# Turning q as plain values and splitting it behind the turn, with q and k-and-v tiles in alternation

## The chip, the core and the metric

The kernel runs on one core of a Trainium2 chip. A core has a matrix engine (TensorE, in the profile PE, with its weight loads as PEld), a vector engine (VectorE, DVE), an engine for activation functions and copies (ScalarE, ACT), a general-purpose engine (GpSimd, POOL) and one that issues transfers (SyncE, SP). They run side by side and wait for each other through semaphores. Data lie in SBUF (128 partitions); TensorE writes its results to PSUM, from where ScalarE and VectorE read them. The metric is the time of one execution on the device, in microseconds (us). Each instruction of one execution was recorded by the hardware profiler; that record is the trace, and its summary the profile page.

## The reference, cut to what matters

One encoder layer for 1024 tokens of 1024 channels, in float32: a half-step feed-forward block, then attention and a state-space part (SSD) side by side on the same projection, an output projection, a second feed-forward block and a gated embedding, each with a layer norm. The change touches the projection to q, k and v, and the normalisation and rotation of q and k:

```python
u = x @ w_in[i]
q, k, v, z, xs, bm, cm, dt_raw = jnp.split(u, SPLIT_POINTS, axis=-1)
qf = _rms(q.reshape(B, S, N_Q_HEADS, HEAD_DIM).astype(jnp.float32), q_norm[i])
kf = _rms(k.reshape(B, S, N_KV_HEADS, HEAD_DIM).astype(jnp.float32), k_norm[i])
qh = _apply_rope(qf, cos, sin).astype(x.dtype)
kh = _apply_rope(kf, cos, sin).astype(x.dtype)
vh = v.reshape(B, S, N_KV_HEADS, HEAD_DIM)
att_out = _block_attention(qh, kh, vh)
```

There are 8 q heads and 2 k and v heads of 64 channels; `_rms` divides each head of each token by its root mean square, and `_apply_rope` turns pairs of channels by an angle that depends on the token. `xs`, `bm` and `cm` (the x/B/C part) go through a short convolution and into the SSD part.

## The kernel before

**Precision.** A float32 product is computed as three products of a shorter type (`F32R`): each operand is split into a leading part hi (a rounded copy) and the rest lo (the difference), and lo-hi, hi-lo and hi-hi are added in PSUM (`mm3`, L116 to L123). `split_into` (L107) makes such a pair: a copy on ScalarE (L108) and a subtraction on VectorE (`lo`, L87). Both run for every weight block and every activation that goes into a product.

**Memory.** PSUM is used through two pools of buffers: `big`, two buffers of 1024 columns (`psb`, L41 and L55), and `sm`, four buffers of 512 (`pss`). A tile that is asked for waits until a buffer of its pool is free, which is when all that read it have run. Split weight blocks live in `ring` (ten buffers, L46). Raw weights land in `raw` buffers, of which there are two in this stage (L1606), by a DMA that SP issues (L94).

**Order.** The whole kernel is traced under `in_order` for TensorE (L1932): its instructions run in the order in which the program names them. On the other engines a scheduler chooses the order at compile time, except where `behind(engine)` ties what follows behind the last instruction named so far on that engine.

**The stage.** Just ahead of it `z_part` computes six tiles of z and loads and splits the q weights (`q_weights`). `qkv_part` (L841) then works in tiles of 128 tokens, t = 0 to 7. The q loop calls `qq(t)`: 24 matmuls of 512 columns into an `sm` buffer. The k-and-v loop calls `kv(t)`: 24 matmuls of 272 columns (128 of k, 128 of v, 16 of dt). After each product comes `step`, which does three things: it takes the oldest waiting *turn* from the list `late`, if more than `keep` of them wait (1 in the q loop, 2 in the k-and-v loop); it runs the *front* of this tile; and it runs the *back* of the tile before.

- `norm` (L862), in the front of both: a square on ScalarE (L865), a sum over each head on VectorE (L867), a scale and an added constant (L868), and the power -1/2 on GpSimd (L870).
- `rope` (L873), in the back: a Newton step for the root (L129 to L132), the product with it (L877, the last reader of the `sm` buffer), and the rotation (L883 to L886) with tables `T`. The tables are products of cosine and sine with the norm's weights, made on VectorE (L859); k's take the place of q's after the first k-and-v tile.
- `q_back` (L920): the rotated q is split into `qs`, per head 64 columns of hi beside 64 of lo (ScalarE L923, VectorE L87). Its turn transposes the 8 heads, 128 x 128 each, so that hi lies over lo in the partitions, into one `big` buffer (L929), and a copy of 1024 columns takes it to `Q` (L930).
- `kv_back` (L904): `rope` writes k twice side by side into `kn`; the turn transposes the 2 heads into an `sm` buffer (L911), and a copy (L913) and a subtraction (L87) split them into `K`.

Attention then multiplies `Q` (hi over lo) with `K`'s hi and lo (L1192). Behind the two loops, `xbc_gemm(0)` computes x0, the first of eight blocks of the x/B/C part, into a `big` buffer, in two halves of 24 matmuls; after each half two of the four steps in `pend` run (L960), which work off the turns that are left. `xbc_part` then reads x0 in a convolution (L992, L997) and goes on with x1 (L1002), into a `big` buffer again. The k-and-v weights are loaded and split in two parts (`kv_weights`, L812) with the last two q tiles, into `ring`; those of x/B/C in `xbc_weights` (L964), at their use.

## Time and profile before

| | |
|---|---|
| time, three runs | median 1938.63 us (1938.40 to 1939.19) |
| the profiled execution | 1938.82 us |
| its span, first to last instruction | 1937.0 us |
| mean granted clock of TensorE | 0.998 |
| transposes of q (L929) | 64, each 272 ns by the trace, from 718.7 to 759.5 us |
| transposes of k (L911) | 16, each 272 ns, from 762.7 to 784.3 us |

The span runs from the first to the last instruction; the rest of the execution's time, 1.8 us, lies around it. Times in the trace count from the span's start. A matmul's duration is longer than the distance to the next one's start, since matmuls overlap; what a group costs is read from the chain, where the pieces follow each other without overlap. Rows of groups give line, engine, operation, output and input with their shapes and count, then busy us and mean ns of one, then the idle time in front of them and what ended it. Rows of a timeline give start, length, engine, line and operation, and in brackets the idle time in front. In the rows of one line or tile, the three numbers are the least, median and greatest duration in ns.

### The profile page before, as it was taken

The page shows a single profiled execution, that of the slowest core. Times are in us where ns is not written, and L with a number is a line of the kernel's source. Part 1 is how long each engine was busy: PE and PEld are TensorE (multiplying, and loading weights), DVE is VectorE, ACT ScalarE, POOL GpSimd, SP SyncE. Part 2 cuts the span into 40 slices and gives each one's busy share as a digit, 9 for nine tenths or more (in the row PEclk, how much of TensorE's full clock was granted, in tenths as well). Part 3 has the DMA queues.
Part 4 walks back from the last instruction along what each step waited for, and adds up shares of the span by engine and source line. Part 5 has one row for each costly group of instructions (what it writes and reads, how often), then busy time and mean ns, then how long its engine had stood idle before and what let it go on. Part 6 is the DMA issues. An engine that isn't in the chain of part 4 may idle for free.

```text
span 1937.0 us, 25655 instructions
## 1 busy us (share of the span) xinstructions
PE 1926.7 (99%) x9130; PEld 1605.8 (83%) x9130; DVE 1524.2 (79%) x2362; ACT 877.5 (45%) x1502; POOL 418.2 (22%) x308
## 2 busy tenths in 40 slices
PE   9999999999999999999999999999999999999998
PEld 7888888888888889888888888888888888888886
DVE  7977777767678658758998888997787686877698
ACT  7433333334444224538897877633333333444311
POOL 0144544430001032001131001014444540001011
PEclk9999999999999999999999999999999999999999
DMA  8434554549866111241002663254544539976022
GB/s 307 134 127 156 189 186 147 196 155 392 279 218 219 61 44 47 88 126 63 6 1 90 218 211 126 92 173 144 184 177 165 188 118 358 333 261 224 27 78 97
DMA packets 147713, 310.34 MB, mean 160 GB/s; under 512 B 18128, under 2 KB 30800, under 8 KB 147584
## 3 DMA queue, kind: packets, MB, share of 16 engines
q1 hardware_dynamic: 147584, 308.69, 45.6%
q8 instruction: 72, 1.18, 0.3%
q14 instruction: 57, 0.47, 0.1%
HBM read 217.21 MB, written 91.42 MB: 159 GB/s over the span
## 4 chain that ended last, share of the span: by engine, by line
PE 99%; DVE 1%; DVEq 0%; issue 0%; ACT 0%
PE sm L122 56%; PE big L519 12%; PE sm L519 9%; PE big L122 6%; PE big L1192 3%; PE sm L1214 3%; PE sm L1229 2%; PE sm L1230 1%; PE sm L639 1%; PE sm L1410 1%; PE sm L1309 1%; PE sm L1320 1%; PE big L224 0%; PE big L929 0%; PE sm L224 0%; PE big L1725 0%
## 5 line engine op out<-in xcount | busy, mean ns | idle before, releaser
L122 PE MATMUL sm<-xh,blk 128*128 128x512 f32 x1424 | 439.8, 389 | 0.0
L122 PEld LDWEIGHTS sm<-xh,blk 128*128 128x128 f32 x1424 | 267.3, 188 | 55.3
L122 PE MATMUL sm<-xl,blk 128*128 128x512 f32 x736 | 283.8, 389 | 0.0
L122 PE MATMUL sm<-blk,xl 128*128 128x512 f32 (+2 forms) x704 | 208.1, 369 | 0.0
L108 ACT CAST blk<-raw 128x512 fp32r<-128x512 f32 (+1 forms) x168 | 101.1, 611 | 216.5 <-PE sm L122 135.3
L87 DVE TENSOR_TENSOR blk<-raw,blk 128x512 fp32r<-128x512 f32 (+1 forms) x168 | 141.6, 846 | 52.2 <-ACT blk L108 51.8
L108 ACT CAST blk<-s 128x512 fp32r<-128x512 f32 x172 | 105.7, 622 | 153.5 <-PE sm L122 126.0
L87 DVE TENSOR_TENSOR blk<-s,blk 128x512 fp32r<-128x512 f32 x176 | 141.8, 809 | 40.6 <-ACT blk L108 38.5
L178 POOL TENSOR_TENSOR ln_k<-ln_k,mhalf 128x1 f32<-128x1 f32 x32 | 37.8, 1185 | 578.2 <-DVE ln_k L177 562.0
L122 PEld LDWEIGHTS sm<-xl,blk 128*128 128x128 f32 x736 | 138.1, 188 | 28.8
L122 PE MATMUL sm<-blk,xh 128*128 128x512 f32 (+2 forms) x448 | 158.1, 373 | 0.0
L122 PEld LDWEIGHTS sm<-blk,xl 128*128 128x128 f32 x704 | 127.8, 188 | 20.8
L267 POOL TENSOR_TENSOR s<-raw 128x512 f32<-128x512 f32 x34 | 57.8, 1701 | 382.0 <-DVE blk L87 355.0
L519 PE MATMUL big<-xh 128*128 128x512 f32 x576 | 138.8, 390 | 0.0
L87 DVE TENSOR_TENSOR xh<-blk,xh 128x1024 fp32r<-128x1024 f32 x78 | 95.3, 1222 | 50.8 <-ACT xh L465 43.3
L465 ACT CAST xl<-blk 128x1024 fp32r<-128x1024 f32 x76 | 80.2, 1055 | 113.2 <-PE sm L519 45.1
L465 ACT CAST xh<-blk 128x1024 fp32r<-128x1024 f32 x78 | 82.2, 1054 | 107.1 <-PE big L519 45.4
L87 DVE TENSOR_TENSOR xl<-blk,xl 128x1024 fp32r<-128x1024 f32 x76 | 92.8, 1221 | 43.3 <-ACT xl L465 38.1
L519 PEld LDWEIGHTS big<-xh 128*128 128x128 f32 x576 | 107.8, 188 | 22.3
L519 PE MATMUL big<-xl 128*128 128x512 f32 x480 | 115.7, 390 | 0.0
L122 PE MATMUL sm<-xET2h,blk 128*128 128x512 f32 x352 | 108.3, 389 | 0.0
L122 PE MATMUL sm<-xET3h,blk 128*128 128x512 f32 x352 | 108.3, 389 | 0.0
(358 smaller groups left out, 4112.4 us busy)
## 6 DMA issues: line engine op xcount, KB each, us to landing
raw<-in_wi_dram SPq DMA_DIRECT2D x81, 512.0 KB
blk<-hS SPq DMA_DIRECT2D x154, 256.0 KB
hS<-h SPq DMA_DIRECT2D x88, 256.0 KB
wr<-in_wo_dram SPq DMA_DIRECT2D x44, 512.0 KB
blk<-wT SPq DMA_DIRECT2D x88, 256.0 KB
hS<-sg SPq DMA_DIRECT2D x66, 256.0 KB
wT<-wr SPq DMA_DIRECT2D x66, 256.0 KB
blk<-in_wo_dram SPq DMA_DIRECT2D x66, 256.0 KB
```

The costliest lines, as they stand in the source:

```text
L87: (eng or self.nc.vector).tensor_tensor(out=out, in0=full, in1=hi.bitcast(F32), op=ALU.subtract)
L108: self.nc.scalar.copy(out=b[:, 0, :n], in_=src)
L122: self.nc.tensor.matmul(ps, lhsT=a, rhs=b, start=(i == 0), stop=(i == n - 1))
L178: nc.gpsimd.tensor_tensor(out=r, in0=v, in1=self.mhalf[:, :1], op=ALU.pow)
L267: lambda: G.tensor_tensor(out=s1, in0=a21, in1=a22, op=ALU.add),
L465: A.copy(out=b[:, :, 0], in_=r)
L519: nc.tensor.matmul(ps[q], lhsT=b[:, 0, x, cut], rhs=b[:, 1, y], start=j == i == 0, stop=j == NP - 1 and i == 2)
L639: nc.tensor.matmul(o, lhsT=pT[t // 4][k][:, i, c], rhs=we[n][k][:, j], start=k + i + j == 0, stop=k + i == 2)
L1192: nc.tensor.matmul(ps[:, n * 512:(n + 1) * 512], lhsT=Q[:, h, q0:q0 + P], rhs=K[:, h // 4, j, n * 512:(n + 1) * 512], start=j == 0, stop=j ...
L1214: nc.tensor.transpose(out=pt[:, k], in_=pr[:, kk * P:(kk + 1) * P], identity=self.ident)
L1229: nc.tensor.matmul(po, lhsT=vw, rhs=pth[k // 4][:, k % 4], start=k == 0, stop=False)
L1230: nc.tensor.matmul(po, lhsT=vw, rhs=ptl[k // 4][:, k % 4], start=False, stop=k == KD - 1)
```

## The change

- `q_back` no longer splits in front of the turn. The turn transposes the plain rotated q, two heads (2 x 64 channels) at a time, into half of a `big` buffer: four transposes. Behind it, two ScalarE copies of 64 partitions round the even and the odd heads into `Q`, and two subtractions on VectorE write lo into the other 64 partitions. For odd heads lo lies over hi; the sum over the partitions in attention is the same.
- `norm` for q makes eight squares of one head each, with the sum from ScalarE's accumulator; VectorE's sum goes. For k it stays.
- The two loops become one: tile t of q, then tile t of k and v. `step` keeps 1 throughout; without a front it does nothing where no turn waits.
- k's turn takes a `big` buffer in place of an `sm` one.
- k's tables are made in front of the loop, on GpSimd, in place in the cosine and sine tables.
- `kv_weights` runs in front of the loop, in three loads of 3, 3 and 2 blocks; six blocks lie in a pool of their own (`wkvp`), two in `ring`.
- The weights of x0 are loaded and split in front of q's last step, behind what ScalarE and VectorE have been given by then; those of x1 behind the loop in the same way.
- Buffer counts: `qn` of q 4 (was 2), `kn` 2 (was 4), `qs` gone, k's square and rotation in small tiles of their own.

```diff
@@ -809,13 +809,11 @@
         self.nc.sync.dma_start(out=t, in_=self.I[key].broadcast_to([P, n]))
         return t
 
-    def kv_weights(self, part):
-        if part == 0:
-            self.wkv = []
-        for k in ((0,), (3, 6))[part]:
-            n = min(3, KD - k)
-            r = self.raw(self.I["wkv"][:, k * 272:(k + n) * 272], n * 272)
-            self.wkv += [self.split(r[:, i * 272:(i + 1) * 272], 272) for i in range(n)]
+    def kv_weights(self, ks, pool):
+        r = self.raw(self.I["wkv"][:, ks[0] * 272:(ks[-1] + 1) * 272], len(ks) * 272)
+        for i, k in enumerate(ks):
+            b = pool.tile([P, 2, 272], F32R, name="wkv") if k < 6 else self.ring.tile([P, 2, 512], F32R, name="blk")
+            self.wkv.append(self.split_into(b, r[:, i * 272:(i + 1) * 272], 272))
 
     def kv(self, t, xT):
         ps = self.pss()
@@ -843,6 +841,7 @@
         Q, K, V = self.qkv
         tabs = c.enter_context(tc.tile_pool(name="tabs", bufs=1))
         wk = c.enter_context(tc.tile_pool(name="qwork", bufs=2))
+        kvp = c.enter_context(tc.tile_pool(name="wkvp", bufs=6))
         cs = tabs.tile([P, NT, HD], F32, name="cs")
         sn = tabs.tile([P, NT, HD], F32, name="sn")
         nc.sync.dma_start(out=cs, in_=I["cs"])
@@ -861,10 +860,14 @@
 
         def norm(ps, nh):
             v = ps.rearrange("p (h d) -> p h d", d=HD)
-            sq = wk.tile([P, nh, HD], F32, name="sq")
-            nc.scalar.activation(out=sq, in_=v, func=AF.Square)
+            sq = wk.tile([P, nh, HD], F32, name="sq" if nh == NQ else "ksq")
             ss = self.small.tile([P, 16], F32, name="ss")[:, :nh]
-            nc.vector.reduce_sum(ss, sq, axis=AX.X)
+            if nh == NQ:
+                for h in range(nh):
+                    nc.scalar.activation(out=sq[:, h], in_=v[:, h], func=AF.Square, accum_out=ss[:, h:h + 1])
+            else:
+                nc.scalar.activation(out=sq, in_=v, func=AF.Square)
+                nc.vector.reduce_sum(ss, sq, axis=AX.X)
             nc.vector.tensor_scalar(out=ss, in0=ss, scalar1=1.0 / HD, scalar2=RMS_EPS, op0=ALU.mult, op1=ALU.add)
             r = self.small.tile([P, 16], F32, name="qr")[:, :nh]
             nc.gpsimd.tensor_tensor(out=r, in0=ss, in1=self.mhalf[:, :nh], op=ALU.pow)
@@ -873,7 +876,7 @@
         def rope(v, nh, m, ss, r, nm, t):
 
             self.newton(r, ss, nh)
-            qn = wk.tile([P, nh, HD], F32, name="qn")
+            qn = wk.tile([P, nh, HD], F32, name="qn", bufs=4) if nh == NQ else wk.tile([P, nh, HD], F32, name="kr", bufs=1)
             nc.vector.tensor_tensor(out=qn, in0=v, in1=r.unsqueeze(2).broadcast_to([P, nh, HD]), op=ALU.mult)
             T1, T2 = (x[:, t] for x in T[nm])
             H2 = HD // 2
@@ -882,10 +885,10 @@
                 i = slice((1 - a) * H2, (2 - a) * H2)
                 nc.vector.tensor_tensor(out=m[:, :, o], in0=qn[:, :, i], in1=T2[:, o].unsqueeze(1).broadcast_to([P, nh, H2]), op=ALU.mult)
             nc.vector.tensor_tensor(out=qn, in0=qn, in1=T1.unsqueeze(1).broadcast_to([P, nh, HD]), op=ALU.mult)
-            if nm == "q":
+            if nh == NQ:
                 nc.vector.tensor_tensor(out=qn, in0=qn, in1=m, op=ALU.add)
                 return qn
-            kn = wk.tile([P, NKV, 2, HD], F32, name="kn", bufs=4)
+            kn = wk.tile([P, NKV, 2, HD], F32, name="kn")
             a, b = (x.unsqueeze(2).broadcast_to([P, NKV, 2, HD]) for x in (qn, m))
             nc.vector.tensor_tensor(out=kn, in0=a, in1=b, op=ALU.add)
             return kn
@@ -906,7 +909,7 @@
             kn = rope(*st, "k", t)
 
             def turn():
-                pt = self.pss()[:, :NKV * P].rearrange("p (g t) -> p g t", g=NKV)
+                pt = self.psb()[:, :NKV * P].rearrange("p (g t) -> p g t", g=NKV)
                 for g in range(NKV):
                     nc.tensor.transpose(out=pt[:, g], in_=kn[:, g].rearrange("p a d -> p (a d)"), identity=self.ident)
                 hi, lo = (K[:, :, j, t * P:(t + 1) * P] for j in range(2))
@@ -918,25 +921,25 @@
             return norm(ps, NQ)
 
         def q_back(t, st):
-            qs = wk.tile([P, NQ, 2, HD], F32R, name="qs", bufs=4)
             qn = rope(*st, "q", t)
-            nc.scalar.copy(out=qs[:, :, 0], in_=qn)
 
             def turn():
-                pt = self.psb().rearrange("p (h t) -> p h t", t=P)
-                qv = qs.bitcast(F32)
-                for hh in range(NQ):
-                    nc.tensor.transpose(out=pt[:, hh], in_=qv[:, hh].rearrange("p a d -> p (a d)"), identity=self.ident)
-                nc.scalar.copy(out=Q[:, :, t * P:(t + 1) * P], in_=pt)
+                pt = self.psb()[:, :512].rearrange("p (h t) -> p h t", t=P)
+                for hp in range(NQ // 2):
+                    nc.tensor.transpose(out=pt[:, hp], in_=qn[:, 2 * hp:2 * hp + 2].rearrange("p h d -> p (h d)"), identity=self.ident)
+                both = [(slice(e * HD, (e + 1) * HD), slice((1 - e) * HD, (2 - e) * HD), Q[:, e::2, t * P:(t + 1) * P]) for e in range(2)]
+                for mine, other, q in both:
+                    nc.scalar.copy(out=q[mine], in_=pt[mine])
+                for mine, other, q in both:
+                    self.lo(q[other], pt[mine], q[mine])
             late.append(turn)
-            return qs[:, :, 1], qn, qs[:, :, 0]
 
         backs, los = [], []
 
         def step(t, ps, front, back, keep=1):
 
 
-            if len(late) > keep or not front:
+            if len(late) > keep or late and not front:
                 late.pop(0)()
             st = front(t, ps) if front else None
             if los:
@@ -947,22 +950,32 @@
                 backs.append(lambda: back(t, st))
 
         tables("q", HD ** -0.5)
+        for t_, nm in ((cs, "kn"), (sn, "kns")):
+            w = self.bcast(tabs, f"w_{nm}", nm, HD)
+            nc.gpsimd.tensor_tensor(out=t_, in0=t_, in1=w.unsqueeze(1).broadcast_to([P, NT, HD]), op=ALU.mult)
+        T["k"] = (cs, sn)
+        self.wx, self.wkv = [], []
+        for ks in ((0, 1, 2), (3, 4, 5), (6, 7)):
+            self.kv_weights(ks, kvp)
+        def wx(j):
+            r = self.raw(self.I["wx"][j])
+            with self.behind(mybir.EngineType.Activation), self.behind(mybir.EngineType.DVE):
+                self.wx.append([self.split(r[:, i * 512:(i + 1) * 512]) for i in range(2)])
+
         for t in range(NT):
             ps = self.qq(t, xT)
-            if t >= NT - 2:
-                self.kv_weights(t - NT + 2)
+            if t == NT - 1:
+                wx(0)
             step(t, ps, q_front, q_back)
-        for t in range(NT):
-            ps = self.kv(t, xT)
-            step(t, ps, kv_front, kv_back, 2)
-            if t == 0:
-                tables("k", 1.0)
+            step(t, self.kv(t, xT), kv_front, kv_back)
+        wx(1)
         self.pend += [lambda: step(NT, None, None, None)] * 4
         self.x0 = self.xbc_gemm(0, xT, 1)
         assert not late and not backs and not los
 
     def xbc_weights(self, j):
-        return [b.rearrange("p l (k c) -> p l k c", c=P) for b in self.wload(self.I["wx"][j])]
+        blocks = self.wx[j] if j < len(self.wx) else self.wload(self.I["wx"][j])
+        return [b.rearrange("p l (k c) -> p l k c", c=P) for b in blocks]
 
     def xbc_half(self, w, xT, h, ps):
         self.mm3(ps, [((w[k // 4][:, 0, k % 4], w[k // 4][:, 1, k % 4]), tuple(x[:, k % 4] for x in xT[h][k // 4])) for k in range(KD)])
```

## The prediction

> **What bounds the kernel now.** I read the page's busy shares and chain first, then who TensorE waits for, then the chain in order of time from 690 to 880 us, where the change lies.
>
> ```profile
> PE 1926.7 (99%) x9130; PEld 1605.8 (83%) x9130; DVE 1524.2 (79%) x2362; ACT 877.5 (45%) x1502; POOL 418.2 (22%) x308
> PE 99%; DVE 1%; DVEq 0%; issue 0%; ACT 0%
> PE big L634 <- DVE s L631: 1.2, 1, 1.2
> ```
>
> TensorE (PE) is busy 99% of the span and is 99% of the chain that ended last; the only wait of it that is listed is 1.2 us at the start. So a transpose that goes is worth its own time, and nothing on another engine is worth anything unless PE comes to wait for it.
>
> ```profile
> 738.75 5.46 PE sm L122 x24
> 744.20 0.87 PE big L929 x8
> 759.81 3.00 PE sm L122 x24
> 762.81 0.22 PE sm L911 x2
> 772.78 5.49 PE big L122 x24
> 778.26 0.44 PE sm L911 x4
> 778.70 5.47 PE big L122 x24
> 784.17 0.44 PE sm L911 x4
> 784.61 21.82 PE big L122 x96
> ```
>
> These are pieces of the chain: start, length, what. A q tile's product takes 5.46 us, its eight transposes (L929) 0.87, a k-and-v tile's product 3.00, its two transposes (L911) 0.22. No piece has a gap behind it. The last five rows are the end of the stage: the first x/B/C product (x0) in two halves, each followed by two k turns, and then the next product (x1) at once.
>
> **Part by part. Transposes.** Four instead of eight per tile. q is plain f32 behind the change as k is now, so four k transposes are the row: 0.44. Removed: 8 x (0.87 - 0.44) = 3.44 us, all on the path. This is the whole gain; no other matmul goes or comes.
>
> **The turn's PSUM buffers.** The k turns move from `sm` (four buffers) to `big` (two buffers of two banks, line 41). In the loop that is covered: turns of q and k take the two in alternation, and each has a product of 3 to 5.5 us between itself and the next. At the end it is not. x0 holds one `big` buffer from its first matmul until its convolution has read it. With the new `step` (keep 1 throughout) two tiles are left behind x0's first half, k of tile 6 and q of tile 7, and both need the other buffer; the order of PE is fixed (`in_order`), so q7's transposes wait until k6 is copied and split out. Behind x0's second half stands k7's turn in that buffer, and x1, which also takes a `big` tile, waits in the same way. Before, x1 found that buffer free. What the wait costs is shown by the k turns of now:
>
> ```profile
> 766.07 0.22 PE sm L911 x2
> 766.33 0.37 ACT L913 CAST K<-sm 128x256 fp32r<-128x256 f32 x1 [2.42 <-PE sm L911]
> 766.86 0.42 DVE L87 TENSOR_TENSOR K<-sm,K 128x256 fp32r<-128x256 f32 x1
> 769.30 0.22 PE sm L911 x2
> 769.96 0.43 DVE L87 TENSOR_TENSOR K<-sm,K 128x256 fp32r<-128x256 f32 x1
> 774.33 0.42 DVE L87 TENSOR_TENSOR K<-sm,K 128x256 fp32r<-128x256 f32 x1
> 780.85 0.75 DVE L87 TENSOR_TENSOR K<-sm,K 128x256 fp32r<-128x256 f32 x2
> ```
>
> From the end of the transposes to the end of the split: 766.29 to 767.28 is 0.99 us, 769.52 to 770.39 is 0.87, 772.78 to 774.75 is 1.97 (the split stood behind others on VectorE), and for the pair of 778.70, 781.60, so 2.90. Each of the two waits lies between 0.87 and 2.90. I take 1.3 for q7's (about the mean of the three single turns, 1.28) and 1.8 for x1's (nearest to 1.97: beside it stand x/B/C weight splits, and the convolution starts). Together **+3.1**.
>
> **What q costs on ScalarE and VectorE.** These rows are of 697 to 773 us, by shape, and below them other stages' nearest shapes.
>
> ```profile
> L867 DVE TENSOR_REDUCE ss<-sq 128x8 f32<-128x512 f32 x8 | 5.5, 684 | 4.3 <-ACT sq L865 4.2
> L87 DVE TENSOR_TENSOR qs<-qn,qs 128x512 fp32r<-128x512 f32 x8 | 5.5, 688 | 2.1 <-ACT qs L923 2.1
> L923 ACT CAST qs<-qn 128x512 fp32r<-128x512 f32 x8 | 5.0, 620 | 11.6 <-DVE qn L886 11.6
> L930 ACT CAST Q<-big 128x1024 fp32r<-128x1024 f32 x8 | 8.1, 1018 | 4.1 <-PE big L929 4.1
> L865 ACT ACTIVATE sq<-sm 128x512 f32<-128x512 f32 x8 | 4.8, 599 | 21.1 <-PE sm L122 21.1
> L1236 ACT COPY a_raw<-sm x16: 577/582/587, 900.1 to 1057.5; 64x512 f32<-64x512 f32 x16
> L1237 DVE TENSOR_TENSOR a_raw<-sm,a_raw x16: 672/690/696, 901.3 to 1058.2; 64x512 f32<-64x512 f32 x16
> L1303 ACT ACTIVATE xs<-xb,sdt x112: 331/334/358, 1062.6 to 1143.2; 128x64 f32<-128x64 f32 x112
> L1484 ACT ACTIVATION_READ_ACCUMULATOR ysq<-y x16: 185/186/194, 1121.8 to 1169.0; 128x1 f32 x16
> ```
>
> VectorE per q tile: the reduction (0.68) goes, one split (0.69) becomes two of half the partitions (2 x 0.69): even. ScalarE: 0.60 + 0.62 + 1.02 = 2.24 becomes 2 x 0.58 + the eight squares with their accumulator reads, at most 8 x (0.33 + 0.19) = 4.2, at least the 0.60 of one square. It is idle more than half of this stage, so the sum of it costs nothing; only the delay counts, because the squares begin the chain of a q tile. I take 2.4 us for the eight: the rows' durations less the overlap of neighbours. The Trainium skill (ScalarE: Activation LUTs, "What ACT_TABLE_LOAD costs") gives an instruction with immediate operands 186 ns plus 0.833 ns an element, neighbours overlapping by about 93 ns. By that a square of 64 is an estimated 0.15 us from start to start and eight with reads about 1.9; the sum above would be the same.
>
> **Is q ready when its turn comes?** The chain of a tile behind its product:
>
> ```profile
> 702.56 0.60 ACT L865 ACTIVATE sq<-sm 128x512 f32<-128x512 f32 x1 [3.52 <-PE sm L122]
> L877 DVE TENSOR_TENSOR qn<-sm,qr 128x512 f32<-128x512 f32 x8 | 5.5, 691 | 0.7
> L883 DVE TENSOR_TENSOR sq<-qn,T 128x256 f32<-128x256 f32 x16 | 6.1, 420 | 0.2
> 704.23 1.65 POOL L870 TENSOR_TENSOR qr<-ss,mhalf 128x8 f32<-128x8 f32 x1 [0.63 <-DVE ss L868]
> 747.23 3.22 POOL L870 TENSOR_TENSOR qr<-ss,mhalf 128x8 f32<-128x8 f32 x1 [5.14 <-DVE ss L868]
> 709.95 0.69 DVE L886 TENSOR_TENSOR qn<-qn,sq 128x512 f32<-128x512 f32 x1
> ```
>
> Now q0's product ends at about 702.5 (its square starts at 702.56), its rotated value is there at 710.64, 8.1 us later. Behind the change the squares add 1.8 (2.4 for 0.6) and the reduction's 0.7 goes: 9.2 us with nobody in the way. In the loop a q turn comes after its k-and-v product, an older turn, the next q, another turn and the next k-and-v: 3.0 + 0.4 + 5.5 + 0.2 + 3.0 = 12.1 us (now three q products, some 16.4). Margin 2.9 us. For q7 it is 3.0 + 0.4 + 5.5 + 0.2 = 9.1, and with the buffer wait of 1.3 above, 10.4: margin 1.2. So at the forecast q7's lateness hides in the buffer wait.
>
> **Load of VectorE.** The alternation mixes q's slack with k's hurry:
>
> ```profile
> 690.00:697.07 7.07, 7.07 (x40) 6.04 (x39) 1.38 (x2) 2.28 (x4) 0.75 (x1) 1.00 0.10 37
> 719.47:744.83 25.36, 25.36 (x131) 21.33 (x130) 20.82 (x54) 11.00 (x19) 7.94 (x4) 1.00 0.09 23
> 744.83:772.80 27.97, 27.97 (x228) 27.97 (x227) 25.30 (x110) 12.44 (x30) 8.27 (x8) 1.00 0.15 48
> ```
>
> The columns are stage, length, then busy us of PE, PEld, DVE, ACT, POOL. VectorE is busy 20.8 of 25.4 us in four q tiles and 25.3 of 28.0 in the k part: 82% and 90%. A pair takes PE 5.46 + 3.00 + 0.44 + 0.22 = 9.1 us; I estimate VectorE's work on it at 7.5 to 8.6, from these rows: a quarter of 20.8 is 5.2, some weight splits among it, an eighth of 25.3 is 3.2, with tails of q and more weight splits among it, and a little is to be added for operations that wait on each other. It keeps up, narrowly.
>
> **Edits I cost at nothing.** The k tables become two GpSimd operations, in place, in POOL's idle time ahead of the stage (busy 0.75 of 7.07 us from 690 to 697); VectorE's two go. The k-and-v weights and the x weights:
>
> ```profile
> 658.08 0.80 SPq L94 DMA_DIRECT2D raw<-in_wkv_dram x2
> 661.55 0.74 ACT L108 CAST blk<-raw 128x272 fp32r<-128x272 f32 x2 [2.82 <-DMA raw<-in_wkv_dram]
> 742.56 38.72 SPq L94 DMA_DIRECT2D raw<-in_wx_dram x7
> ```
>
> Two of three k-and-v loads already go out at 658 us, and two splits of eight are done by 663; the rest waited for `ring` buffers of wq. With buffers of their own six follow at once, the last two take the ring's two free ones, and k0's product needs them only at 702.5. That puts six more splits on VectorE among the layer norms from 660 us on; from 690 to 697 it is busy 1.38 of 7.07 us, so they are covered. If the cover were gone, k0 would wait by what is missing, at most the eight splits' 3 us. The loads pass SP's stores of z and y, which are not on the path. The wx loads move from 742 forward; their splits stand behind q6's chain on VectorE, so are done some 9.2 + 2 x 0.69 = 10.6 us behind q6's product, and x0 starts 9.1 + 3.0 + 0.4 = 12.5 behind it. The bounds of these are 0 and +3, taken 0. Smaller `kn` (two buffers) is freed by a turn before the tile after next.
>
> **Sum.** -3.44 + 1.3 + 1.8 = -0.34 us. The profiled execution took 1938.82 us (span 1937.0 and 1.8 around it), the median of three is 1938.63. So 1938.3 to 1938.5: **1938.4**.
>
> **Rivals.** *The waits are short or absent* (the scheduler has k6 and k7 out at once, or the buffers are not what I read): 1938.8 - 3.4 = 1935.4; with 0.87 twice, 1937.1. For it: copies started 0.04 us behind the transposes in the rows above. Against: a buffer that x0 holds cannot be had. Chance 0.20.
>
> *VectorE falls behind* (slower). If a pair takes it longer than 9.1 us, the lag grows through eight pairs, eats q's margin of 2.9 us, and PE stands at each later turn. At 10.3 us a pair: 8 x 1.2 - 2.9 = 6.7 us, so 1945.1. It decides from 9.5. For it: 90% busy in the k part, in-order waits for POOL, and POOL's root taking 3.22 us where VectorE was dense against 1.65 where it idled. Against: the sum of 7.5 to 8.6. The Trainium skill (GPSIMD Engine Reference, "8. Key points") says that GpSimd shares its SBUF interfaces with VectorE and contends with its instructions of two SBUF inputs; those POOL rows agree. By that rule each q chain is 1.2 us longer here, inside the loop's margin and just at q7's. Chance 0.12.
>
> *A late first weight or x0 weight*: +1 to +3 on the sum, 1939.5 to 1941.5. Chance 0.08. The forecast itself (1937.1 to 1940) 0.60.
>
> **Chances.** A measurement of this kernel tells about 0.2%, 3.9 us, from no change: faster means under 1934.8, slower above 1942.5. Even the whole gain (3.44) stays short of that, so faster needs something that I don't see: 0.05. Slower is most of VectorE's rival: 0.11. Same: 0.84. Range 1935.2 (gain without waits) to 1941.5 (a late weight).
>
> **What would show it.** Right: four transposes of 0.44 us in each q turn; two idle times of PE of 0.9 to 2.9 us, before q7's transposes and before x1's first matmul, both ended by VectorE's split of K; no gap elsewhere from 697 to 770. Wrong: gaps of PE at turns in the loop, ended by L886 (VectorE behind); a gap before the first k-and-v product (weights); or no gap at the end (buffers misread). If the time is under 1935, the gain has a part that is not the transposes.

## The result, and the profile after

The changed kernel takes **1941.64 us** (median of 22 runs, 1939.70 to 1942.91); the kernel before, on the same chip, 1938.55 (median of 22). The ratio is 1.0016, 95% interval 1.0009 to 1.0022: 3 us slower, clear of 1 but inside the 0.2% that the prediction takes as the least that a measurement tells from no change. (One of the 22 runs of the kernel before took 8057 us; the others lie from 1938.22 to 1939.26.) The forecast was 1938.4, its range ended at 1941.5. The profiled execution of the changed kernel took 1940.64 us, its span 1938.9. Lines behind the change are 13 higher than before (L1738 was L1725).

From its page, the busy line; and from its view of waits, all that it lists for TensorE (PE): in total, times, longest.

```profile
PE 1923.8 (99%) x9098; PEld 1603.5 (83%) x9098; DVE 1529.2 (79%) x2360; ACT 881.1 (45%) x1622; POOL 418.3 (22%) x310
```

```profile
PE big L929 <- DVE qn L889: 2.1, 1, 2.1
PE big L122 <- DVE pm L1124: 1.2, 1, 1.2
PE big L634 <- DVE s L631: 1.2, 1, 1.2
PE sm L1322 <- DVE state L1339: 1.0, 1, 1.0
PE sm L122 <- DVE accr L1518: 0.3, 1, 0.3
```

There are 32 matmuls fewer, and PE is busy 2.9 us less. In their place stand the two waits that were forecast, q7's transposes (L929) and x1's first matmul (L122 of `big`); nothing waits in the loop or before the first k-and-v product. The last two rows are new and lie far behind the change: `state` and `accr` belong to the SSD part.

Three rows of the timeline of each kernel show where the two part: the last transposes ahead of the stage (L224), the first x transposes (L1030, now L1043), the first transposes of the output product (L1725, now L1738). First before, then after.

```profile
696.03 1.03 PE L224 MATMUL big<-ident,acc 128*128 128x128 f32 x8
...
806.26 1.03 PE L1030 MATMUL sm<-ident,conv 128*128 128x128 f32 x8
...
1175.62 1.91 PE L1725 MATMUL big<-ident,acc 128*128 128x128 f32 x16
```

```profile
695.60 1.03 PE L224 MATMUL big<-ident,acc 128*128 128x128 f32 x8
...
806.18 1.04 PE L1043 MATMUL sm<-ident,conv 128*128 128x128 f32 x8
...
1177.45 1.91 PE L1738 MATMUL big<-ident,acc 128*128 128x128 f32 x16
```

From the end of the first row to the end of the second, **the stage**, it is 110.2 us before and 110.6 after; from there to the end of the third, **the stretch behind it**, 370.2 and 372.1. Up to the end of the first row the changed kernel is 0.4 us ahead, and from the end of the third to the end of the span both take 759.5. So 0.4 us is lost where the change lies, and 1.9 where nothing was changed: on every engine the instructions of that stretch stand in the same order in both kernels.

**In the stage** (changed kernel, timeline, TensorE around the two waits, and VectorE and ScalarE ahead of the first):

```profile
773.60 1.29 DVE L87 TENSOR_TENSOR blk<-raw,blk 128x512 fp32r<-128x512 f32 x2
774.33 0.38 PE L914 MATMUL big<-ident,kn 128*128 128x128 f32 x2
774.75 0.37 ACT L916 CAST K<-big 128x256 fp32r<-128x256 f32 x1 [2.18 <-PE big L914]
774.80 0.69 DVE L887 TENSOR_TENSOR qn<-qn,T 128x512 f32<-128x512 f32 x1
...
775.59 0.42 DVE L87 TENSOR_TENSOR K<-big,K 128x256 fp32r<-128x256 f32 x1
775.93 0.68 DVE L889 TENSOR_TENSOR qn<-qn,sq 128x512 f32<-128x512 f32 x1
...
776.76 0.63 PE L929 MATMUL big<-ident,qn 128*128 128x128 f32 x4 [2.05 <-DVE qn L889]
...
782.70 0.38 PE L914 MATMUL big<-ident,kn 128*128 128x128 f32 x2
784.30 0.47 PE L122 MATMUL big<-xh,blk 128*128 128x512 f32 x1 [1.22 <-DVE pm L1124]
```

k6's turn (L914) starts at 774.33, its split of K is done at 776.01, and q7 could have had the buffer; but its rotation (L889) ends only at 776.61, because VectorE split two blocks of x weights (773.60) in the midst of it. So the first wait is set by VectorE's queue. The second ends at the operation that follows K's split on VectorE (pm, L1124); whether the buffer sets it is for an experiment. From the start of the turn before to the start of what waits it is 2.43 and 1.60 us, where it is 0.13 behind a k turn without a wait (rows of an experiment below): 3.8 more together, against 8 x (0.87 - 0.44) = 3.4 saved.

**Behind it** VectorE waits for the store of y to `yd`. The timeline's rows of SP's issues (SPq: start, length of the issue) and of the waiting instruction, before and after:

```profile
1080.07 0.57 SPq L1412 DMA_DIRECT2D yd<-y  x1
...
1096.84 0.34 SPq L1412 DMA_DIRECT2D yd<-y  x1
1097.94 0.32 SPq L1665 DMA_DIRECT2D y<-accr  x1
1098.94 0.69 DVE L1400 TENSOR_TENSOR y<-xb,dsk 128x512 f32<-128x512 f32 x1 [1.03 <-DMA yd<-y]
```

```profile
1080.49 1.22 SPq L1425 DMA_DIRECT2D yd<-y  x1
...
1097.26 0.34 SPq L1425 DMA_DIRECT2D yd<-y  x1
1098.37 1.21 SPq L1678 DMA_DIRECT2D y<-accr  x1
1100.78 0.69 DVE L1413 TENSOR_TENSOR y<-xb,dsk 128x512 f32<-128x512 f32 x1 [2.44 <-DMA yd<-y]
```

The same store, issued at the same place, lands 1.4 us later (the buffer of y is free again at 1100.78 for 1097.26, before 1098.94 for 1096.84), and VectorE then brings `state` late to TensorE. What is new beside it shows in the DMA view by queue (packets, MB, share of 16 engines), after, 1096.5 to 1099.5 us; before, q8 has no packet in that window:

```profile
q8 instruction: 1, 0.02, 2.9%
```

Queue q8 of kind "instruction" moves 71 packets, 1.16 MB, in the whole execution: one packet of 16 KB for each 256 of TensorE's 2 x 9098 instructions. It is TensorE's code. With 64 instructions fewer (32 transposes with their weight loads) each later packet comes elsewhere: in the trace at 1080.4 and 1097.8 us, before at 1073.1 and 1092.4. The Trainium skill (Runtime: NRT & Kernel Launch, "Instruction fetch mechanics") says that code comes in blocks of 16 KiB or 256 instructions over a DMA queue of the engine's own, mostly hidden. The trace agrees on the block, and TensorE indeed doesn't wait for it. That the store lands late because of the packet beside it is so far only a guess from the two traces.

### The profile page after: what moved, and what is told of

It is laid out like the page before. It is cut to its first block, busy times and chain, and to the rows that moved or that the text cites. A ratio compares the mean times of both kernels' runs of the same rounds, so it can differ in the third digit from the quotient of the medians.

```text
span 1938.9 us, 25722 instructions
## 1 busy us (share of the span) xinstructions
PE 1923.8 (99%) x9098; PEld 1603.5 (83%) x9098; DVE 1529.2 (79%) x2360; ACT 881.1 (45%) x1622; POOL 418.3 (22%) x310
## 3 DMA queue, kind: packets, MB, share of 16 engines
q8 instruction: 71, 1.16, 0.2%
## 5 line engine op out<-in xcount | busy, mean ns | idle before, releaser
L122 PE MATMUL sm<-xh,blk 128*128 128x512 f32 x1424 | 440.1, 390 | 0.0
L122 PEld LDWEIGHTS sm<-xh,blk 128*128 128x128 f32 x1424 | 267.4, 188 | 55.3
L122 PE MATMUL sm<-xl,blk 128*128 128x512 f32 x736 | 284.1, 390 | 0.0
L122 PE MATMUL sm<-blk,xl 128*128 128x512 f32 (+1 forms) x608 | 190.4, 381 | 0.0
L122 PEld LDWEIGHTS sm<-xl,blk 128*128 128x128 f32 x736 | 138.2, 188 | 28.5
L122 PE MATMUL sm<-blk,xh 128*128 128x512 f32 (+2 forms) x400 | 144.3, 383 | 0.3 <-DVE accr L1518 0.3
L122 PEld LDWEIGHTS sm<-blk,xl 128*128 128x128 f32 x608 | 112.8, 188 | 20.7
L122 PE MATMUL sm<-xET3h,blk 128*128 128x512 f32 x352 | 108.4, 389 | 0.0
L122 PE MATMUL sm<-xET2h,blk 128*128 128x512 f32 x352 | 108.4, 389 | 0.0
```

What stands on the lines that cost most here:

```text
L122: self.nc.tensor.matmul(ps, lhsT=a, rhs=b, start=(i == 0), stop=(i == n - 1))
```

## The experiments

First theory, **code**: the 1.9 us come of where the code packets fall. Its rival, **own**: they come of the change itself, wherever the packets fall. For the waits in the stage, theory **buffer** stands against theory **VectorE** (its backlog sets them, the buffers only where they show). Each kernel has its median and range of 11 runs (where not said), the ratio to the kernel before with its 95% interval, and stage and stretch from its trace, measured from last start to last start of the groups above (before: 110.23 and 370.24; after: 110.58 and 372.14).

| kernel | us (range) | ratio (interval) | code as in | stage | stretch | wait for yd |
|---|---|---|---|---|---|---|
| a_code | 1940.20 (1939.24-1941.53) | 1.0009 (1.0000-1.0017) | before | 110.55 | 370.58 | 1.02 |
| b_code | 1940.56 (1940.03-1941.08) | 1.0010 (1.0001-1.0019) | after | 110.24 | 371.47 | 2.06 |
| b_ctrl | 1939.32 (1938.78-1940.14) | 1.0003 (0.9994-1.0012) | before | 110.23 | 370.70 | 1.02 |
| b_turn (5 runs) | 1945.27 (1944.27-1945.61) | 1.0032 (1.0020-1.0045) | after | 115.34 | 371.83 | 2.17 |
| a_norm_code (5 runs) | 1945.11 (1944.10-1946.21) | 1.0033 (1.0020-1.0045) | before | 116.26 | 370.42 | 1.00 |
| a_kend | 1939.33 (1938.30-1941.47) | 1.0005 (0.9996-1.0014) | after | 109.10 | 372.04 | 2.43 |
| a_end | 1938.57 (1937.79-1939.30) | 0.9999 (0.9990-1.0008) | after | 108.65 | 372.04 | 2.64 |
| a_end_code | 1937.96 (1936.80-1938.28) | 0.9994 (0.9986-1.0003) | before | 108.67 | 370.39 | 0.96 |
| a_end_prep_code | 1937.68 (1937.29-1938.14) | 0.9995 (0.9986-1.0004) | before | 108.69 | 370.55 | 0.95 |
| a_pool_code (10 runs) | 1943.41 (1942.57-1944.82) | 1.0025 (1.0016-1.0034) | before | 114.82 | 370.16 | 1.01 |
| a_end_pool_code | **1936.42** (1935.92-1937.09) | 0.9988 (0.9979-0.9997) | before | 107.18 | 370.38 | 1.02 |
| a_end_pool | 1937.10 (1936.10-1937.71) | 0.9990 (0.9981-0.9999) | after | 107.14 | 372.06 | 2.65 |
| a_fill_code | 1938.86 (1938.54-1939.71) | 1.0001 (0.9992-1.0010) | before | 110.68 | 370.42 | 0.97 |
| after_again (1 run) | 1942.18 | | after | 112.18 | 371.86 | 2.62 |

### The place of the code packets: a_code, b_code, b_ctrl

The kernels' warm-up, matmuls of zeros at the very start, is cut finer; a_code starts from the changed kernel, the others from the kernel before.

```diff
-        for i in range(14):
-            nc.tensor.matmul(o, lhsT=zero[:, :P], rhs=zero[:, :512], start=True, stop=True)
+        for i in range(46):
+            nc.tensor.matmul(o[:, :156], lhsT=zero[:, :P], rhs=zero[:, :156], start=True, stop=True)
```

In b_code it is 110 of 64 columns, in b_ctrl 142 of 50.

> The changed kernel with its 14 warm-up matmuls of 512 columns cut into 46 of 156 (7176 columns for 7168): 64 more TensorE instructions, as many as the change took away, so every later code load of TensorE stands at the instruction where it stood before the change. Theory code (the 1.9 us lost between 1058 and 1115 us come of a code load that meets the stores and loads of y and accr): that loss goes, no 3.4 us store of yd near 1097 us, time 1938.8 to 1939.7 and the runs lie close together. Rival own (the loss is the change's own, by the order or timing it gives, wherever the code loads fall): 1941.6 as the changed kernel, the same waits at 1100 us.

> The kernel before with its 14 warm-up matmuls of 512 columns cut into 110 of 64 (7040 columns for 7168): 192 more TensorE instructions, which is 64 fewer modulo the 256 of one code load, so the later code loads stand where those of the changed kernel stand; nothing else is touched. Theory code: 1940 to 1942, runs spread by some 3 us, and a load or store of y or accr near 1060 to 1100 us lands later than before. Rival own: 1938.5 with runs within 1 us.

> The kernel before with its 14 warm-up matmuls of 512 columns cut into 142 of 50 (7100 columns for 7168): 256 more TensorE instructions, one whole code load, so the later code loads stand where those of the kernel before stand. It is the control of the run with 110: by theory code it has no loss between 1058 and 1115 us and is 1938.6 to 1939.5 (up to 0.9 for an early code load among the first loads of data, which cost the run with 110 some 0.7 us ahead of 690 us). If cutting the warm-up by itself costs the 1.9 us, it is 1940.5 as that run.

b_code, in which nothing else is changed, is 1.2 us slower than its control b_ctrl; its stretch is 371.47 us against 370.70. a_code stands 1.6 us above the kernel before in its comparison (1938.64), the changed kernel 3.1 in its own: 1.5 us less, with a stretch of 370.58 against 372.14. Over all kernels the two groups don't touch: with packets in the old place the stretch is 370.2 to 370.7 us and the wait for yd 0.95 to 1.03; in the new place 371.5 to 372.1 and 2.06 to 2.65. **Code holds**, its rival falls. The size varies: in the profiles of b_code and b_ctrl only 0.8 us of the difference lie in the stretch and 0.6 lie ahead of the stage (its first row ends at 697.80 and 697.20), where only the cut of the warm-up differs. Of the 1.9 us, a_code gets back 1.6. And a_code's median was expected at 1938.8 to 1939.7 and is 1940.2, and its runs lie in two groups, 1939.2 to 1940.2 and 1940.9 to 1941.5: this was still open.

### Parts of the change alone: b_turn, a_norm_code

b_turn gives the kernel before only the new `q_back` (as in the change's diff; `qn` with four buffers), with the tiles in the old order and the k turns in `sm`. a_norm_code takes only the squares of the change back, with the 46 warm-up matmuls:

```diff
-            if nh == NQ:
-                for h in range(nh):
-                    nc.scalar.activation(out=sq[:, h], in_=v[:, h], func=AF.Square, accum_out=ss[:, h:h + 1])
-            else:
-                nc.scalar.activation(out=sq, in_=v, func=AF.Square)
-                nc.vector.reduce_sum(ss, sq, axis=AX.X)
+            nc.scalar.activation(out=sq, in_=v, func=AF.Square)
+            nc.vector.reduce_sum(ss, sq, axis=AX.X)
```

> The kernel before with one part of the change alone: q is turned as plain values, four transposes, and split behind the turn; tiles in the old order, k turned in sm, weights in the ring as before, k tables on VectorE. The transposes' term alone, with no buffer of the turn held by x0: stage of the first products to the end 3.4 us shorter. TensorE has 64 instructions fewer, so code loads stand as in the changed kernel. Theory code: 1935.1 plus 1 to 3, so 1936 to 1938. Rival own (the alternation or the k turns in big bring the loss behind the stage): 1935.1.

> The changed kernel with q's sum of squares as before (one square of 128x512 on ScalarE, the sum on VectorE) and with the 46 warm-up matmuls: both TensorE and ScalarE then have as many instructions as in the kernel before, so the code loads of both stand in the old place. The run with the 46 alone had times in two groups (1939.2 to 1940.2 and 1940.9 to 1941.5). If ScalarE's code loads make the second group, this run is 1938.8 to 1939.5 and close together; if not, 1940.2 with the same spread. The stage by itself: q's chain is 1.1 us shorter on ScalarE and 0.7 longer on VectorE, so the wait of q7's turn changes by no more than 0.5 from 2.1.

Both were far off: the stage is 5.1 and 6.0 us longer than before, not 3.4 shorter or unchanged. Waits of TensorE in a_norm_code:

```profile
PE big L122 <- DVE K L87: 3.8, 1, 3.8
PE big L925 <- DVE qn L885: 2.8, 1, 2.8
```

Each of the two kernels has eight operations of 0.68 us, some 5.5 us, more on VectorE in this stage than the changed kernel: the sums over heads (from the view of groups of b_turn, 697 to 778 us):

```profile
L87 DVE TENSOR_TENSOR Q<-big,Q 64x512 fp32r<-64x512 f32 x16 | 11.0, 689 | 0.7 <-ACT Q L929 0.3
L867 DVE TENSOR_REDUCE ss<-sq 128x8 f32<-128x512 f32 x8 | 5.5, 682 | 3.8 <-ACT sq L865 3.8
```

So VectorE has no slack at the end of this stage, and the eight squares on ScalarE, which I had weighed as a delay of q's chain alone, are what pays for the second subtraction. A part of the 5 to 6 us is not VectorE's, though, but a fall of TensorE's clock, shown further below: by the sums by window the granted clock was 0.55 and 0.59 of full from 786 to 794 us in a_norm_code, and in b_turn 0.61 from 756 to 760, 0.74 and 0.83 from 764 to 772. Worked out as there, that is some 6.8 us at half speed and up to 3.4 us lost in each. The rest, the waits, speaks for theory VectorE.

### The waits at the end: a_kend, a_end, a_end_code, a_end_prep_code

a_kend gives the k turns of the last two tiles buffers of `sm`; a_end does so with q7's turn too and puts it behind x0's second half; a_end_code adds the 46 warm-up matmuls, and a_end_prep_code moves a chain of small VectorE operations (`ssd_prep`) from x0's convolution to x1's.

```diff
-                pt = self.psb()[:, :NKV * P].rearrange("p (g t) -> p g t", g=NKV)
+                pt = (self.psb() if t < NT - 2 else self.pss())[:, :NKV * P].rearrange("p (g t) -> p g t", g=NKV)
...
-                pt = self.psb()[:, :512].rearrange("p (h t) -> p h t", t=P)
+                pt = (self.psb() if t < NT - 1 else self.pss())[:, :512].rearrange("p (h t) -> p h t", t=P)
...
-        self.pend += [lambda: step(NT, None, None, None)] * 4
+        self.pend += [lambda: step(NT, None, None, None), lambda: None] + [lambda: step(NT, None, None, None)] * 2
...
-            if j in (0, 2):
+            if j in (1, 2):
                 next(prep, None)
```

The first pair is a_kend, the first three are a_end, and the last comes on top of a_end_code in a_end_prep_code.

> The changed kernel with the k turns of the last two tiles in sm in place of big and nothing else. x1's first matmul then need not wait for k7's copy (1.2 us gone). q7's transposes no longer wait for k6's buffer; if that buffer was what held them, their 2.1 us go too and the stage is 3.3 us shorter than the changed kernel's; if q7's own rotation holds them (the trace names it), 1.5 to 2.1 of that wait stay and the stage is 1.2 to 1.8 shorter. Code loads stand as in the changed kernel, so the loss of 1.9 us behind the stage stays: 1941.6 less 1.2 to 1.8, so 1939.8 to 1940.4; 1938.3 if both waits go.

> The changed kernel with the k turns of the last two tiles and the q turn of the last tile in sm in place of big, and that q turn put behind x0's second half: both end-of-stage waits (2.1 and 1.2 us) should be gone. If they are all that stood against the transposes, the stage ends 3.3 us earlier and the time is 1938.3 (changed kernel less 3.3); by theory code the loss behind the stage stays at 1 to 3 us with wide runs; by theory own it stays at 1.9. If TensorE waits elsewhere instead (another buffer of sm, a weight of x1), the gain is under 2.

> The changed kernel without its two waits at the end of the stage (the kernel with the last k and q turns in sm) and with the 46 warm-up matmuls that put the code loads back in the old place. That kernel had a stage 1.6 us shorter than before and lost 1.9 us behind it: by theory code the second goes, so 1938.57 less 1.4 to 1.9, about 1937, faster than both kernels. By theory own it stays at 1938.6.

> The changed kernel with the last k and q turns in sm, the 46 warm-up matmuls, and the chain of small operations on dt (some 7 us of VectorE, 19 operations) begun with x1's convolution in place of x0's. Theory VectorE: x0's convolution ends about 2 us earlier, so the wait of 1.0 for it goes and nothing else changes ahead of it: 1937.0. Against it: the products of that chain on TensorE come with x2, and if the chain isn't done there, TensorE waits for VectorE some us: 1939 to 1943.

In a_kend x1 follows k7's turn at once (timeline), and the stage is 1.48 us shorter than the changed kernel's: the second wait was the buffer's. q7's wait stays at 2.0, ended by its rotation: the first wasn't. The median, 1939.33, lies half a microsecond under what was expected, and the runs are again in two groups (1938.30 to 1939.76, 1940.46 to 1941.47).

```profile
782.95 0.38 PE L914 MATMUL sm<-ident,kn 128*128 128x128 f32 x2
783.08 0.48 PE L122 MATMUL big<-xh,blk 128*128 128x512 f32 x1
```

a_end has neither wait, but not the 3.3 us either: its stage is 1.93 us shorter than the changed kernel's, since TensorE now waits for VectorE at two other places (0.4 for k7's sum, 0.9 for x0's convolution). That its median still falls by 3.1, near the forecast, is not by the stage alone: its runs have no slow group any more, which the last experiments explain. Moving the small operations (a_end_prep_code) leaves the wait for the convolution at 1.0 and the stage at 108.69; the expected gain of a microsecond didn't come, so those operations were not what held it. a_end_code against a_end is the code packets again: the stretch falls by 1.65, the median by 0.6 where 1.4 or more was expected; in the two profiles 0.7 us is lost again ahead of the stage (697.64 for 696.98 at the end of the first row).

### VectorE relieved: a_pool_code, a_end_pool_code, a_end_pool

Four subtractions of x weights, 2.6 us, go from VectorE to GpSimd: in a_pool_code beside the 46 warm-up matmuls, in a_end_pool_code on top of a_end_code, in a_end_pool with the 14 warm-up matmuls again.

```diff
-                self.wx.append([self.split(r[:, i * 512:(i + 1) * 512]) for i in range(2)])
+                self.wx.append([self.split(r[:, i * 512:(i + 1) * 512], eng=nc.gpsimd if j else None) for i in range(2)])
...
-        blocks = self.wx[j] if j < len(self.wx) else self.wload(self.I["wx"][j])
+        blocks = self.wx[j] if j < len(self.wx) else self.wload(self.I["wx"][j], eng=self.nc.gpsimd if j == 2 else None)
```

> The changed kernel with the 46 warm-up matmuls and with four subtractions of x weights (blocks of x1 and x2) on GpSimd in place of VectorE, 2.6 us of VectorE's work that stood among q7's rotation and K's splits. Compared with the run with the 46 alone (waits of 2.1 before q7's transposes and 1.2 before x1; 1940.2). Theory VectorE (the waits at the end of the stage are VectorE's backlog, the buffers only say where it shows): both waits shrink, together from 3.3 to 0.5 to 1.5, time 1937.5 to 1939. Theory buffer (the wait is the way of K through the one free buffer): q7's 2.1 shrinks to no less than 1.3 and x1's 1.2 stays; together 2.5, time 1939.4.

> The changed kernel with the last k and q turns in sm, the 46 warm-up matmuls, and the same four subtractions on GpSimd. Without the GpSimd part TensorE still waited 0.4 us for k7's sum and 1.0 us for x0's convolution, and the stage was 1.6 us shorter than before of the 3.4 that the transposes give. Theory VectorE: 2.6 us less of its work takes both waits away, the stage is 3.0 to 3.4 us shorter than before, time 1936 to 1936.8 (1937.96 less 1.2 to 1.8). If a buffer or a weight holds TensorE instead, 1937.5 to 1938.

> The kernel of 1936.42 us (last turns in sm, four subtractions on GpSimd) with the 14 warm-up matmuls of the changed kernel again: TensorE has 64 instructions fewer, so its code loads stand beside the y stores as in the changed kernel. Theory code: VectorE waits 2.0 to 2.7 us for the store near 1095 us in place of 1.02, time 1937.5 to 1938.2. Rival own: 1936.4.

a_end_pool_code has no wait in the stage at all and a stage 3.05 us shorter than before: theory VectorE held there, with the whole gain of the transposes but 0.4 (not followed up). Its median is 2.4 us under the kernel before, 0.9988 (0.9979 to 0.9997); with a_end_pool it is the only version whose interval lies under 1, and this too is inside the 0.2%. a_end_pool has the longer stretch again; its median is 0.7 us higher, less than the 1.1 expected, and its profiled run, 1937.71, was its slowest. So a packet beside the store cost up to 1.7 us in the profiled runs; that it costs less in others is likely, but no other was profiled.

a_pool_code went the other way: waits of 3.3 and 2.5 us in place of 2.1 and 1.2, and a clock of 0.65 and 0.92 from 786 to 794 us, which costs up to 1.7 us more. The timelines of a_pool_code and, below, of a_code show why:

```profile
770.92 5.06 POOL L87 TENSOR_TENSOR blk<-raw,blk 128x512 fp32r<-128x512 f32 x4
770.98 1.25 DVE L129 TENSOR_TENSOR rs_t<-qr 128x2 f32<-128x2 f32 x1
...
774.95 1.64 DVE L886 TENSOR_TENSOR sq<-qn,T 128x256 f32<-128x256 f32 x2
```

```profile
770.90 0.16 DVE L129 TENSOR_TENSOR rs_t<-qr 128x2 f32<-128x2 f32 x1
...
773.21 0.76 DVE L886 TENSOR_TENSOR sq<-qn,T 128x256 f32<-128x256 f32 x2
```

While GpSimd worked on its four subtractions, VectorE operations with two inputs in SBUF took 1.25 us for 0.16 and 1.64 for 0.76; those that read PSUM did not (L880 beside them takes 0.68 us in both). They stand in and around q7's chain, and k6's split of K, with which TensorE's wait ended, stands behind it. In a_end_pool_code the same GpSimd work lies at the same place (5.10 us from 771.20) and slows the same operations as much (1.26 and 1.69 us). But q7's turn comes behind x0's second half there, so TensorE didn't come to wait for them. The rule of the Trainium skill that the prediction cited (GPSIMD Engine Reference, "8. Key points") agrees with these rows.

### Two groups of times: after_again, a_fill_code

> The changed kernel once more, for a second profile. By theory code a code load of TensorE again stands beside the first y store near 1080 us and beside the one near 1097 us, that store's issue takes 0.9 to 1.3 us in place of 0.57, and VectorE waits 2.0 to 2.7 us for the one near 1097. The time lies anywhere from 1939.7 to 1942.9; if it is over 1941, the trace says where the slower of its runs lose their further microsecond.

This second run of the changed kernel has the same two waits, 2.1 and 1.2 us, and yet a stage 1.6 us longer. Its timeline, and below it its sums by window (start:end, length, busy us of PE, PEld, DVE, ACT, POOL, then the granted clock, DMA share, GB/s):

```profile
776.98 0.63 PE L929 MATMUL big<-ident,qn 128*128 128x128 f32 x4 [2.05 <-DVE qn L889]
777.36 0.55 PE L122 MATMUL big<-xh,blk 128*128 128x512 f32 x1
777.70 1.05 PE L122 MATMUL big<-xl,blk 128*128 128x512 f32 x2
778.56 0.63 PE L122 MATMUL big<-xh,blk 128*128 128x512 f32 x1
```

```profile
774.00:778.00 4.00, 1.95 (x12) 1.50 (x11) 3.97 (x9) 0.73 (x2) 0.00 (x0) 0.95 0.38 129
778.00:782.00 4.00, 4.00 (x12) 3.09 (x12) 3.70 (x10) 2.35 (x5) 0.00 (x0) 0.62 0.44 133
```

Behind the wait the matmuls come 0.43 us apart for 0.23 in the first profile (three from 777.46 to 778.15), and the granted clock is 0.62 of full from 778 to 782. Worked out as half speed, that is 0.05 x 4 / 0.5 + 0.38 x 4 / 0.5 = 3.4 us, and 1.7 us lost. In the first profile the clock stays at 1.00. The changed kernel's runs bear it out: 5 with a mean granted clock of 0.999 have a median of 1940.40 us and all lie under 1941, 16 with 0.998 one of 1941.78 and all lie above it, as does the one with 0.997. (A mean of 0.998 alone shows no fall: the profile of the kernel before has it too, with a clock of 1.00 through the stage.) The Trainium skill (TensorE: Matmul & The Clock Gate, "What's actually happening") says that the clock falls to half after an idle window of some 3.4 us, which runs freely. The trace agrees on the length and the depth; but here a gap of 2.05 us, shorter than that window, was enough in some runs.

How long a gap must be, these runs don't settle. In a_pool_code's profile the clock stayed at 1.00 behind the wait of 3.28 us and fell at the one of 2.50; in b_turn's it fell at waits of 0.91 and 1.10 us in close succession. In the clock records of the four traces with a fall (after_again, b_turn, a_norm_code, a_pool_code) each of the five falls comes a whole number of times 3.413 us behind the clock's first rise (220, 223, 226, 229 and 229 times). So it may be decided by how much of a gap lies in one step of that grid, which would be why the clock stays up behind the same wait in some runs; this was not tested.

a_fill_code is a_code with eight matmuls in the wait, whose result nobody reads, and eight warm-up matmuls fewer (38 of 189 columns):

```diff
+                if t == NT - 1:
+                    o, w = self.pss(), self.xbc_weights(0)
+                    for i in range(8):
+                        nc.tensor.matmul(o, lhsT=w[0][:, 0, 0], rhs=xT[0][0][0][:, 0], start=True, stop=True)
```

> The run of the changed kernel with 46 warm-up matmuls had two groups of times: median 1939.8 where the mean granted clock was 0.999 and 1941.1 where it was 0.997 or 0.998. Here eight matmuls whose result nobody reads stand ahead of q7's transposes (8 x 0.227 = 1.8 us of work in a wait of 2.05 us), and there are eight warm-up matmuls fewer (38 of 189 columns), so the count of TensorE instructions is the same. Theory clock (the wait of 2 us makes the granted clock fall to half for some 3 us in part of the runs, 1.6 us each time): q7's transposes start when they did, the clock stays at 1.00 there, all runs lie in the upper group's place, 1939.2 to 1940.2, median 1939.7. Rival (the spread comes of something else, DMA or the start of the kernel): two groups as before, median 1940.2.

**Clock holds**: with useless work in the wait the runs are one group, 1938.54 to 1939.71; the slow one is gone. The median is 1.3 us under a_code's, lower even than expected, but not all of that is the clock: of the two profiles, in neither of which the clock falls in the stage, a_fill_code's is 0.6 us ahead before the stage begins (696.43 for 696.99 at the end of the first row), where only the warm-up differs.

## Why the prediction was wrong, point by point

- **Transposes.** Right: four in place of eight, each of 272 ns; a_end_pool_code, in which nothing waits, shows a stage 3.05 us shorter, of the 3.44 forecast.
- **The two waits.** Right in place and together: 3.3 us of idle time forecast as 3.1. Singly they were 2.1 and 1.2 for 1.3 and 1.8; that these two errors cancel is luck. Wrong in one reason: q7's margin of 1.2 us was gone. I had put the x weights' splits of VectorE "behind q6's chain"; x2's, tied to nothing, stood within q7's chain, so that q7's lateness did not hide in the wait for the buffer but set the wait. a_kend tells the two waits apart.
- **VectorE's load.** The forecast "even" is right, and no wait came in the loop. But "narrowly" was narrower than I said: eight operations of 0.68 us more (b_turn, a_norm_code) made the stage 5 to 6 us longer than before, up to 3.4 of it by the clock. The rival "VectorE falls behind" names what these two kernels show, not what the change does. The 1.2 us by which GpSimd was to lengthen each q chain have no source in the two rows given, which differ by 1.57, and did not come: its root of q takes 1.64 to 1.74 us in all eight tiles (L873), beside 1.65 in the shorter of those rows.
- **The squares.** Their rows in the changed kernel's timeline start 0.20 us apart with their reads, so eight take 1.6 us, less than the 2.4 taken; the prediction's estimate from the Trainium skill (ScalarE: Activation LUTs, "What ACT_TABLE_LOAD costs") was 1.9.
- **Weights ahead, tables on GpSimd.** Right at nothing: the stage starts no later (695.60 for 696.03) and nothing waits ahead of k0.
- **The step that failed** is the **Sum**: "-3.44 + 1.3 + 1.8 = -0.34 us", which takes a wait to cost its own length and all behind the stage to cost nothing. Where the clock stays up, the stage comes out at +0.4 for this -0.34, since the two waits cost 3.8 and not 3.1. Two terms were missing. (1) A wait of 2.05 us lowers the clock behind it, by the times in most runs: 1.2 us of the median (1941.64 for all runs, 1940.40 for the 5 with a mean clock of 0.999). (2) 64 TensorE instructions fewer move the code packets onto the y stores 300 us later: 1.5 us of the median (changed kernel against a_code), 1.6 of the stretch. With both undone, a_fill_code takes 1938.86 against 1938.78 for the kernel before beside it, ratio 1.0001 (0.9992 to 1.0010): within the error this is the sum as forecast, with some luck, as its profile gains 0.6 us ahead of the stage and loses 0.45 in it. The range reached to 1941.5 for a late weight, a cause that didn't come, and had nothing for these.

## What to carry to other kernels

Price a new wait of a TensorE that never waits at more than its length, and shorten or fill it: here 2.05 us of it halved the clock for 3.4 us in a part of the runs. When instructions go or come on TensorE, the code packets behind them move; a loss of a microsecond in an unchanged part should be tried with a changed count of instructions ahead of it before it is explained. And a gain on the engine that is 99% busy is only kept as far as the next engine can follow: here 2.6 us of VectorE's work had to go too, and the turn that stood in its way had to come later, since GpSimd's help slows VectorE while it lasts.

## What the runs showed of the hardware that was not expected

- A code packet of 16 KB per 256 TensorE instructions, beside a store of 256 KB, lengthened VectorE's wait for that store from 0.95 to 1.03 us to 2.06 to 2.65 (the one near 1097 us in the changed kernel). In the same kernels SP's issue of an earlier store of y, near 1080 us, took 0.82 to 1.49 us for 0.57.
- The granted clock fell to half for 3.4 us behind a gap of 2.05 us, not in every run; in the kernels with no wait over 1.3 us in the stage the times did not go with the mean clock.
- GpSimd's subtractions slowed VectorE's operations with two SBUF inputs while they ran: one of 128x2 took 1.25 us for 0.16, in a_pool_code as in a_end_pool_code (1.26).
